# Two sums of modulation rows in the even layer, moved from TensorE to VectorE

## The chip, the core and the metric

One core of one Trainium2 chip runs one program. The metric is the device time of one execution in microseconds (us). The kernel before has a median of 1068.35 us over three runs (1067.42 to 1072.57). A second figure is the span of one profiled execution, from which all rows below come: 1067.8 us, in an execution that took 1069.53 us.

## What is computed

The reference is a trunk of two layers over 512 tokens of width 1024. What bears on the change is the modulation: for each layer `c_act @ ada_w[layer] + ada_b[layer]` gives 6144 numbers, which are cut into `shift1, scale1, gate1, shift2, scale2, gate2`.

```python
mod = c_act @ ada_w[layer] + ada_b[layer]
shift1, scale1, gate1, shift2, scale2, gate2 = jnp.split(mod, 6, axis=-1)
h = modulate(rmsnorm(x, norm1_w[layer]), shift1, scale1)
...
x = x + gate1[:, None, :] * mix
h2 = modulate(rmsnorm(x, norm2_w[layer]), shift2, scale2)
ffn = hier_moe(h2, ...)
x = x + gate2[:, None, :] * ffn
```

Layer 0 (the even one) mixes by pooling and by chunked attention with eight heads; layer 1 by a state space mixer. After each mixer come 32 experts, of which each token uses two.

## The kernel before

The tokens lie in four tiles of 128. A layer's modulation is made in three parts of 2048 columns by the generator `ada(layer, part, eng)` (line 171): part 0 is shift1 and scale1, part 1 gate1 and shift2, part 2 scale2 and gate2. A part reads a weight matrix of 1024 x 2048 in eight tiles `ada` of 128 x 2048 (1 MB each, line 188), two ahead, and ends a step (`yield`) per tile.

There are two ways to add up. With `eng=None` TensorE multiplies each tile by a column of `ccol` (the activated c), four matmuls a tile into four groups of 32 rows of one PSUM bank (`ada_mm`, line 168). With an engine given, that engine makes a running sum: the first tile times its column of `ccol` (line 204), then each next tile times its column plus the sum so far (line 202), in place. TensorE then multiplies the last tile by ones (line 212), four matmuls in all. `SLACK` (1) empty steps lie between the last sum and this product. Then a bias is added (line 215), and the rows go to DRAM (`modd`) or, in part 0, through transposes `pm` (`mod_cols`, line 306) into columns.

In the even layer the parts (0,1), (0,2) and (1,0) are made beside the attention. `even_mixer` writes its work in one order: projections `pdq`, `pdk`, `pdu` (three passes of matmuls, 24 for each 128 columns), scores `sc` with their softmax on VectorE and ScalarE, transposes `ptr` of the probabilities, values `po`, pooling `py`, and last the output projection `mo`. Between these pieces `fill()` takes so many steps of the generators as the table `FILL` says. Tile then sets a fixed order for each engine from this program order, its dependencies and its buffers; each engine runs that order. The softmax of one pair of heads is eight tiles, each with an addition of the bias with a row maximum (line 685), a negation (687), an exponential on ScalarE (688), a reciprocal (689) and a product (690), giving `pr`.

The tiles `ada` have five buffers (`W8`), which the experts' first weights use after them. A tile's buffer is free when its last reader is done: before, the matmuls of that tile; with a running sum, the sum of the next tile. All loads are issued by SyncE's queue in one fixed order, and a load that waits for its buffer holds what is queued behind it.

After part (0,2) the router's weights are scaled (line 251), for which `mc` is read back from `modd` (line 244). After part (1,0) the row buffer of its bias is free, and `gate1` is loaded into it (line 463); the rows of the output projection's weights are multiplied by it (line 492) and split into a high and a low half (`mow0h` on ScalarE, `mow0l` on VectorE, lines 111 and 112) before `mo` can start. Behind `mo` lie the router and the experts of layer 0, then layer 1.

Of the kernel before, what the change touches and what calls it, by code (L numbers as in the profile page):

```python
# [51 lines left out]
SLACK = 1  # L52
# [24 lines left out]
def trunk_kernel(ctx, tc, x, c, ada_w, ada_b, norm1_w, norm2_w, mix_w_in, pool_w, pool_scale,  # L77
# [4 lines left out]
    V, S, GP, PE, SP = nc.vector, nc.scalar, nc.gpsimd, nc.tensor, nc.sync  # L82
# [7 lines left out]
    def w8(shape, name):  # L90
        return wp.tile(shape, F32, tag="w8", name=name, bufs=W8)
# [10 lines left out]
    def ps(shape=(P, 512), name="ps"):  # L102
        return pp.tile(list(shape), F32, tag="ps", name=name)

    def load_after(ins, first):

        if first is not None:
            tc.add_manual_dep(ins.ins, first.ins.name, SYNC, reason="load_after")
# [56 lines left out]
    def ada_mm(p, k, w, first, last):  # L165

        for q in range(4):
            PE.matmul(p[32 * q:32 * q + 32, :], ccol[:, k:k + 1].to_broadcast([P, 32]), w[:, q * 512:(q + 1) * 512],  # L168
                      start=first, stop=last, skip_group_check=True)

    def ada(layer, part, eng, first=None):


        rows = small.tile([P, D], F32, tag="rows", name=f"adab{layer}{part}", bufs=1)
        b = rows[:, 0:512]
        GP.memset(b, 0.0)
        SP.dma_start(b[0:P:32, :], ada_b[layer, part * 2048:(part + 1) * 2048].rearrange("(b n) -> b n", n=512))
        if part == 2:
            router_loads(layer)
            n2 = rows[:, 512:D]  # L180
            GP.memset(n2, 0.0)
            SP.dma_start(n2[0:64:32, :], norm2_w[layer].rearrange("(b n) -> b n", n=512))
        ws = {}

        def load(k):
            if k < KD:
                ws[k] = w8([P, 2048], f"ada{layer}{part}{k}")
                load_after(SP.dma_start(ws[k], ada_w[layer, k * P:(k + 1) * P, part * 2048:(part + 1) * 2048]), first)

        load(0)  # L190
        load(1)
        p = None
        for k in range(KD):
            load(k + 2)
            yield
            if not eng:
                if not k:
                    p = ps(name=f"pada{layer}{part}")
                ada_mm(p, k, ws.pop(k), k == 0, k == KD - 1)
                continue  # L200
            if k:
                a = eng.scalar_tensor_tensor(ws[k], ws[k], ccol[:, k:k + 1], ws[k - 1], op0=ALU.mult, op1=ALU.add)  # L202
            else:
                a = eng.tensor_scalar(ws[0], ws[0], ccol[:, 0:1], None, op0=ALU.mult)
            if k in PIN:
                tc.keep_in_program_order(a)
        for _ in range(SLACK if eng else 0):
            yield
        if eng:
            p = ps(name=f"pada{layer}{part}")  # L210
            for q in range(4):
                PE.matmul(p[32 * q:32 * q + 32, :], ones[:, 0:32], ws[KD - 1][:, q * 512:(q + 1) * 512], start=True,
                          stop=True, skip_group_check=True)
        m = b
        V.tensor_add(m, p, b)
        if part == 0:
            mod_cols(layer, m)
        elif part == 1:
            SP.dma_start(modd[layer, 1], m[0:P:32, :])
        else:  # L220
            SP.dma_start(modd[layer, 2, 2:4], m[64:P:32, :])
            V.scalar_tensor_tensor(n2, m, 1.0, n2, op0=ALU.add, op1=ALU.mult)
            SP.dma_start(modd[layer, 2, 0:2], n2[0:64:32, :])
            yield from router_prep(layer)
# [5 lines left out]
    def router_loads(layer):  # L230
        d = rt[layer] = {"wr": small.tile([P, KD, NLOG], F32, tag="wr", name=f"wr{layer}", bufs=1)}
        d["mc"] = small.tile([P, 2, KD], F32, tag="mc", name=f"mc{layer}", bufs=1)
        d["lb"] = small.tile([P, NLOG], F32, tag="lb", name=f"lb{layer}", bufs=1)
        GP.memset(d["wr"], 0.0)
        GP.memset(d["lb"], -BIG)
        SP.dma_start(d["wr"][:, :, 0:4], moe_w_group[layer].rearrange("(p k) g -> p k g", k=KD))
        SP.dma_start(d["wr"][:, :, 8:NLOG], moe_w_expert[layer].rearrange("(p k) g e -> p k (g e)", k=KD))
        SP.dma_start(d["lb"][:, 0:4], dap(moe_b_group, 4 * layer, [[0, P], [1, 4]]))
        SP.dma_start(d["lb"][:, 8:NLOG], dap(moe_b_expert, 32 * layer, [[0, P], [1, 32]]))

    def router_prep(layer):
        d = rt[layer]
        for q, off in enumerate((4096, 3072)):
            SP.dma_start(d["mc"][:, q, :], dap(modd, layer * 6144 + off, [[KD, P], [1, KD]]))
        for _ in range(SLACK2):
            yield
        p = ps((P, NLOG), name=f"plb{layer}")
        for k in range(KD):
            PE.matmul(p, d["mc"][:, 1, k:k + 1].to_broadcast([P, P]), d["wr"][:, k, :], start=k == 0, stop=k == KD - 1)
        V.tensor_add(d["lb"], p, d["lb"])  # L250
        V.tensor_mul(d["wr"], d["wr"], d["mc"][:, 0, :, None].to_broadcast([P, KD, NLOG]))
# [51 lines left out]
    def mod_cols(layer, m):  # L303
        p = ps((P, 4, P), name=f"pm{layer}")
        for q in range(4):
            PE.transpose(p[:, q, :], m[:, q * P:(q + 1) * P], ident)
        A = ab[:, layer, 0, :].rearrange("p (b q) -> p b q", b=2)
        B = ab[:, layer, 1, :].rearrange("p (b q) -> p b q", b=2)
        V.scalar_tensor_tensor(A, p[:, :, 64::32].rearrange("p q b -> p b q"), 1.0,
                               n1w[layer].rearrange("p (b q) -> p b q", b=2), op0=ALU.add, op1=ALU.mult)  # L310
        V.tensor_copy(B, p[:, :, 0:64:32].rearrange("p q b -> p b q"))
# [201 lines left out]
    def even_mixer(layer):  # L513
        with ExitStack() as es:
# [217 lines left out]
            order = (0, 1, 4, 5, 6, 2, 7, 3)  # L732
            c_hi, c_lo = ({k: cs[n // 2][:, n % 2, q, :] for n, k in enumerate(order)} for q in range(2))

            adas = [ada(0, 1, None), ada(0, 2, None), ada(1, 0, None)]

            fills = iter(FILL)

# [716 lines left out]
    def odd_mixer(layer, prev):  # L1455
        with ExitStack() as es:
# [25 lines left out]
            with ExitStack() as es2:  # L1482
# [246 lines left out]
                def gnorm(g0):  # L1729
# [14 lines left out]
                    for q in range(2):  # L1744
                        b = tmp(f"gb{g0}{q}")
                        GP.partition_broadcast(b, y[64 * q:64 * q + 1, :])  # L1746
                        for e in range(2):
                            m = 2 * (g0 + q) + e
                            V.scalar_tensor_tensor(gT[m], gT[m], nwcol[:, m:m + 1], b, op0=ALU.mult,
                                                   op1=ALU.mult)  # L1750

                a11, a12 = ada(1, 1, V, prev.gathers[HOLD]), ada(1, 2, V, prev.gathers[HOLD])
                fill = [a11] * (9 + SLACK) + [a12] * (10 + SLACK + SLACK2)
                moe = Moe(layer)
# [62 lines left out]
        return moe  # L1817

    moe = odd_mixer(1, even_mixer(0))
    fw = []  # L1820

# [55 lines left out]
```

## Time and profile before

| what | value |
|---|---|
| median of three runs | 1068.35 us |
| the profiled execution | 1069.53 us |
| its span | 1067.8 us |
| TensorE (PE) busy | 975.3 us, 91% |
| VectorE (DVE) busy | 671.4 us, 63% |
| ScalarE (ACT) busy | 441.1 us, 41% |
| GpSimd (POOL) busy | 175.4 us, 16% |
| mean granted TensorE clock | 0.962 of full speed |
| read from and written to HBM | 254.15 MB and 20.11 MB |

Times in the trace count from the span's start. A row of the timeline gives start, duration, engine, line, operation, out<-in and size; in brackets stands how long the engine was idle before it, and what it had waited for. A matmul's end is modelled, so that two starts tell more than a duration. PE runs its matmuls in the order of the program.

### The profile page before, as it was taken

How to read it: one execution, taken by the hardware profiler on the slowest of the kernel's cores; microseconds unless marked ns; L12 is line 12 of the kernel's file. 1: busy time of each engine (PE TensorE's matmuls, PEld its weight loads, DVE VectorE, ACT ScalarE, POOL GpSimd, SP SyncE). 2: the span in 40 equal slices, each digit the busy share in tenths (PEclk: the TensorE clock that was granted, in tenths of full speed). 3: DMA queues.
4: the chain of work that ended last, by engine and by line, in shares of the span. 5: the costliest groups of instructions: out<-in, count | busy, mean ns of one | idle time of the engine just before them, and what ended most of it. 6: DMA issues, size and time to landing. Idle time of an engine off the chain costs nothing. (4 is left out here: it accounts for less than half of the span.)

```text
span 1067.8 us, 15932 instructions
## 1 busy us (share of the span) xinstructions
PE 975.3 (91%) x5700; PEld 722.0 (68%) x5700; DVE 671.4 (63%) x1508; ACT 441.1 (41%) x893; POOL 175.4 (16%) x252
## 2 busy tenths in 40 slices
PE   5889998898799998899999999999959997999993
PEld 4576654687556656778887887888738776665653
DVE  3424444445564875868986889985874555655864
ACT  4334442315122334437675574665532233222332
POOL 3002110304241123400000200100110004321133
PEclk9899999998899999999999999999969997999997
DMA  9689867698599979747884358654338544899987
GB/s 320 215 290 297 292 218 274 244 366 292 196 376 412 411 245 273 242 104 200 254 236 119 108 150 261 213 139 118 99 120 325 204 160 164 280 412 414 410 251 178
DMA packets 137839, 263.87 MB, mean 247 GB/s; under 512 B 17555, under 2 KB 79975, under 8 KB 132632
## 3 DMA queue, kind: packets, MB, share of 16 engines
q1 hardware_dynamic: 126760, 235.36, 63.3%
q0 software_dynamic: 8928, 20.97, 7.5%
q10 hardware_dynamic: 2064, 6.42, 1.5%
q8 instruction: 49, 0.80, 0.3%
q14 instruction: 38, 0.31, 0.1%
HBM read 254.15 MB, written 20.11 MB: 257 GB/s over the span
## 5 line engine op out<-in xcount | busy, mean ns | idle before, releaser
L1063 PE MATMUL ph<-w,xT 128*64 128x256 f32 (+1 forms) x1152 | 132.1, 374 | 1.5 <-DVE xT L1047 1.2
L1063 PEld LDWEIGHTS ph<-w,xT 128*64 128x64 f32 x1152 | 86.6, 139 | 52.6 <-issue 10.8
L1065 ACT ACTIVATE th<-ph 128x128 f32<-128x128 f32 x34 | 9.4, 277 | 156.3 <-PE pht L1074 131.9
L1084 PE MATMUL pyy<-w,hidT 128*64 128x512 f32 x272 | 65.9, 605 | 4.3 <-ACT hidT L1076 3.8
L1049 ACT ACTIVATE xT<-pxt,mc 128x128 f32<-128x128 f32 x136 | 51.1, 457 | 17.3 <-PE pxt L1042 11.8
L1030 POOL DMA_INDIRECT xg<-xnd,toks x32 | 32.2, 1007 | 150.7 <-PE pxt L1042 123.4
L1089 DVE SCALAR_TENSOR_TENSOR y<-pyy,wsl,gate 128x512 f32<-128x512 f32 x68 | 47.9, 742 | 7.0 <-DMA yd<-y 5.4
L1042 PE MATMUL pxt<-ident,xg 128*128 128x128 f32 x272 | 37.9, 284 | 14.8 <-DVEq L1415 8.5
L1066 DVE SCALAR_TENSOR_TENSOR th<-th,ph 128x128 f32<-128x128 f32 x34 | 9.7, 286 | 60.5 <-ACT th L1065 60.5
L1047 DVE TENSOR_SCALAR xT<-pxt,mc 128x128 f32<-128x128 f32 x136 | 46.6, 403 | 1.4 <-PE pxt L1042 1.4
L1042 PEld LDWEIGHTS pxt<-ident,xg 128*128 128x128 f32 x272 | 34.5, 194 | 15.4 <-issue 15.0
L1631 ACT ACTIVATE ms<-lb,acs 128x128 f32<-128x128 f32 x128 | 40.0, 389 | 10.9 <-DMA lb<-acd 10.9
L1115 DVE TENSOR_TENSOR x<-x,pyc 128x512 f32<-128x512 f32 x48 | 30.4, 681 | 21.1 <-DMA x<-yd,row 16.9
L1727 POOL TENSOR_TENSOR gsum<-gsum,sq 128x512 f32<-128x512 f32 x8 | 11.7, 1458 | 188.6 <-ACT sq L1726 166.2
L1595 DVE SCALAR_TENSOR_TENSOR cvx<-pdx,cw,cvx 128x511 f32<-128x511 f32 (+2 forms) x48 | 35.6, 742 | 0.5 <-ACT cvx L1592 0.5
L1084 PEld LDWEIGHTS pyy<-w,hidT 128*64 128x64 f32 x272 | 16.5, 136 | 28.3 <-issue 19.4
L492 DVE TENSOR_TENSOR sor<-sor,gate 128x1024 f32<-128x1024 f32 x16 | 19.9, 1251 | 21.9 <-DMA sor<-in_ssm_w_out_dram 21.9
L1746 POOL PARTITION_BROADCAST gb<-gy x8 | 9.2, 1151 | 147.6 <-DVE gy L1743 139.0
L1210 POOL DMA_INDIRECT x<-yd,row x16 | 25.4, 1590 | 48.1 <-issue 23.9
L202 DVE SCALAR_TENSOR_TENSOR ada<-ada,ccol,ada 128x2048 f32<-128x2048 f32 x14 | 32.8, 2344 | 0.1
L1107 PE MATMUL pyc<-yh,yot 128*128 128x512 f32 x96 | 25.7, 397 | 1.8 <-DVE yot L1097 1.8
L168 PE MATMUL pada<-ada,ccol 128*32 128x512 f32 x192 | 24.9, 600 | 1.1 <-DMA ada<-in_ada_w_dram 1.1
(1086 smaller groups left out, 2662.2 us busy)
## 6 DMA issues: line engine op xcount, KB each, us to landing
w<-in_moe_w_dram SPq DMA_DIRECT2D x192, 512.0 KB
ada<-in_ada_w_dram SPq DMA_DIRECT2D x40, 1024.0 KB
yd<-y SPq DMA_DIRECT2D x22, 512.0 KB
ada<-in_ada_w_dram SPq DMA_DIRECT2D x16, 512.0 KB
wx<-in_ssm_w_in_dram SPq DMA_DIRECT2D x16, 512.0 KB
wz<-in_ssm_w_in_dram SPq DMA_DIRECT2D x16, 512.0 KB
lb<-acd SPq DMA_DIRECT2D x32, 256.0 KB
sor<-in_ssm_w_out_dram SPq DMA_DIRECT2D x16, 512.0 KB
```

The lines of the kernel that those rows point to most:

```text
L202: a = eng.scalar_tensor_tensor(ws[k], ws[k], ccol[:, k:k + 1], ws[k - 1], op0=ALU.mult, op1=ALU.add)
L1030: d = GP.indirect_dma_start(out=xg, out_offset=None, in_=xnd[:, :], in_offset=bass.IndirectOffsetOnAxis(ap=idx, axis=0), bounds_check=T - ...
L1042: PE.transpose(p[:, q, :], xv[:, 4 * hf + q, :], ident)
L1047: V.tensor_scalar(xT[:, k, :], p[:, q, :], a, b, op0=ALU.mult, op1=ALU.add)
L1049: S.activation(xT[:, k, :], p[:, q, :], AF.Identity, bias=b, scale=a)
L1063: PE.matmul(ph[64 * j:64 * j + 64, n:n + h, :], xT[:, k, 64 * j:64 * j + 64], w13[n][:, :, k, :], start=k == 0, stop=k == KD - 1, skip_gro ...
L1084: PE.matmul(py[64 * j:64 * j + 64], hT[:, 64 * j:64 * j + 64], w2[:, s], start=True, stop=True, skip_group_check=True)
L1089: V.scalar_tensor_tensor(y[:, s], py, self.wsl[:, slot:slot + 1], self.gate2[:, s], op0=ALU.mult, op1=ALU.mult)
L1107: PE.matmul(p, part[2][:, i * P:(i + 1) * P], part[hf][:, q * 512:(q + 1) * 512], start=not sums and n + q == 0, stop=stop and n == len(pa ...
L1115: V.tensor_add(xst["x"][i][:, s], xst["x"][i][:, s], p)
L1595: V.scalar_tensor_tensor(a[:, sh:], p[:, :T - sh], cw[:, tap, ch:ch + 1], a[:, sh:], op0=ALU.mult, op1=ALU.add)
L1631: S.activation(ms[:, h, :], lb[:, h, :], AF.Relu, scale=-1.0, bias=acs[:, cq, 4 * g + h:4 * g + h + 1])
```

## The change

`ada` takes the number of empty steps as an argument. Part (0,1) stays on TensorE. Parts (0,2) and (1,0) become running sums on VectorE, with two and three empty steps ahead of their products by ones.

```diff
-    def ada(layer, part, eng, first=None):
+    def ada(layer, part, eng, first=None, slack=SLACK):
...
-        for _ in range(SLACK if eng else 0):
+        for _ in range(slack if eng else 0):
             yield
...
-            adas = [ada(0, 1, None), ada(0, 2, None), ada(1, 0, None)]
+            adas = [ada(0, 1, None), ada(0, 2, V, slack=2), ada(1, 0, V, slack=3)]
```

The three places where the order matters most follow. First, PE behind the scores of the third pair of heads, from the last matmul of the projection `q3` on; `plb` is the router's bias, `ptr` transposes the probabilities of this pair. Before:

```order
L452 MATMUL pdq_1295<-hhi_179,q3l 128x512
L168 MATMUL pada_1054<-ada_1110,ccol 32x512 x4
L168 MATMUL pada_1054<-ada_1138,ccol 32x512 x4
L168 MATMUL pada_1054<-ada_1210,ccol 32x512 x4
L249 MATMUL plb_1340<-wr_960,mc_961 128x40 x8
L168 MATMUL pada_1360<-ada_1354,ccol 32x512 x4
L168 MATMUL pada_1360<-ada_1356,ccol 32x512 x4
L700 MATMUL ptr_1373<-exch,pr_1215 128x128
```

And in the changed kernel:

```order
L452 MATMUL pdq_1279<-hhi_179,q3l 128x512
L212 MATMUL pada_1309<-ada_1194,ones 32x512 x4
L249 MATMUL plb_1320<-wr_960,mc_961 128x40 x8
L700 MATMUL ptr_1340<-exch,pr_1199 128x128
L700 MATMUL ptr_1344<-exch,pr_1199 128x128 x2
```

Five groups of products became one, which reads the last tile of the sum (0,2), `ada_1194`; everything behind it on PE stands in line.

Second, VectorE in the same place, in the changed kernel: the end of the softmax of the third pair (`mx` row statistics, `pr_1199` and `pr_1200` the probabilities of its two heads).

```order
L685 ISA scs_1267,mx_1266<-sc_1264,strip_1196 128x128
L685 ISA mx_1266 128x1
L202 SCALAR_TENSOR_TENSOR ada_1194<-ada_1194,ccol,ada_1125 128x2048
L689 RECIPROCAL mx_1257<-mx_1257 128x1
L687 TENSOR_SCALAR mx_1266<-mx_1266 128x1
L690 TENSOR_SCALAR pr_1199<-scs_1258,mx_1257 128x128
L689 RECIPROCAL mx_1266<-mx_1266 128x1
L690 TENSOR_SCALAR pr_1200<-scs_1267,mx_1266 128x128
L215 TENSOR_TENSOR adab_957<-pada_1309,adab_957 128x512
```

Of the eight sums of part (0,2) the first five stand ahead of this softmax, among the splits `k3l` and `u2l`; two stand inside it and the last one, shown here, has only five small instructions of the softmax behind it.

Third, PE at the end of the attention: the last matmul of the pooling's projection `u3`, then what follows. Before, the eight products of part (1,0) and the transposes `pm` stood ahead of `pdu` of `u2` and `u3`. Now:

```order
L452 MATMUL pdu_1558<-hhi_179,u3l 128x512
L212 MATMUL pada_1599<-ada_1439,ones 32x512 x4
L306 MATMUL pm_1605<-ident,adab_1331 128x128 x4
L700 MATMUL ptr_1612<-exch,pr_1444 128x128
L700 MATMUL ptr_1616<-exch,pr_1444 128x128 x2
```

On VectorE the first three sums of part (1,0) come behind the router's scaled weights (line 251); the second and third are parted by the low half of `po`, and the other five lie inside the fourth pair's softmax, the last of them (`ada_1439`) behind all its products.

## Rows read from the trace of the kernel before

**Rows 1.** The page's first part: engine, busy us, share of the span, instructions.

```profile
PE 975.3 (91%) x5700; PEld 722.0 (68%) x5700; DVE 671.4 (63%) x1508; ACT 441.1 (41%) x893; POOL 175.4 (16%) x252
```

**Rows 2.** Windows: stretch, its length, busy us per engine, PE clock, DMA share, GB/s.

```profile
100.00:125.00 25.00, 25.00 (x140) 16.25 (x142) 11.67 (x48) 11.89 (x28) 3.40 (x3) 1.00 0.90 306
125.00:150.00 25.00, 24.87 (x144) 15.23 (x140) 10.61 (x41) 10.35 (x29) 0.20 (x1) 1.00 0.64 224
150.00:175.00 25.00, 23.89 (x152) 12.37 (x148) 4.87 (x14) 6.47 (x16) 3.08 (x3) 1.00 0.95 358
```

**Rows 3.** Timeline of PE, attention of the third and fourth pair of heads.

```profile
142.97 0.50 PE L449 MATMUL pdq<-hhi,q3h 128*128 128x512 f32 x1
...
148.64 1.92 PE L168 MATMUL pada<-ada,ccol 128*32 128x512 f32 x16
...
151.35 1.98 PE L249 MATMUL plb<-wr,mc 128*128 128x40 f32 x16
153.26 1.92 PE L168 MATMUL pada<-ada,ccol 128*32 128x512 f32 x16
155.11 1.31 PE L700 MATMUL ptr<-exch,pr 128*128 128x128 f32 x10
...
165.34 1.25 PE L700 MATMUL ptr<-exch,pr 128*128 128x128 f32 x10
...
168.51 2.37 PE L711 MATMUL po<-ptT,vsb 128*64 128x512 f32 x14
170.81 1.12 PE L682 MATMUL sc<-kT,qT 64*128 64x512 f32 x2
```

**Rows 4.** Every sum in layer 1: operation, count, duration ns least/median/most.

```profile
L204 DVE TENSOR_SCALAR ada<-ada,ccol x2: 1273/1276/1279, 490.4 to 639.8; 128x2048 f32<-128x2048 f32 x2
L202 DVE SCALAR_TENSOR_TENSOR ada<-ada,ccol,ada x14: 2335/2343/2353, 497.2 to 672.0; 128x2048 f32<-128x2048 f32 x14
```

**Rows 5.** Timeline of DVE: the softmax of the second pair, first and last instruction.

```profile
115.52 0.69 DVE L685 CUSTOM_DVE_ANT_0 scs<-sc,strip 128x512 f32<-128x512 f32 x1
...
123.38 0.29 DVE L690 TENSOR_SCALAR pr<-scs,mx 128x128 f32<-128x128 f32 x1
```

**Rows 6.** Timeline of DVE: router's weights, values of the third pair, and the gate.

```profile
161.59 0.49 DVE L251 TENSOR_TENSOR wr<-wr,mc 128x320 f32<-128x320 f32 x1 [7.42 <-DMA mc<-modd]
171.55 0.69 DVE L112 TENSOR_TENSOR c<-po,c 128x512 fp32r<-128x512 f32 x1 [9.47 <-ACT c L111]
172.16 0.68 DVE L685 CUSTOM_DVE_ANT_0 scs<-sc,strip 128x512 f32<-128x512 f32 x1
...
185.80 1.23 DVE L492 TENSOR_TENSOR mor<-mor,gate 128x1024 f32<-128x1024 f32 x1 [3.26 <-DMA gate<-modd]
```

**Rows 7.** Timeline of PE, from the end of the modulation to the output projection.

```profile
180.59 0.66 PE L306 MATMUL pm<-ident,adab 128*128 128x128 f32 x4 [3.12 <-DVE adab L215]
181.00 0.49 PE L449 MATMUL pdu<-hhi,u2h 128*128 128x512 f32 x1
...
193.60 1.25 PE L700 MATMUL ptr<-exch,pr 128*128 128x128 f32 x10
...
198.84 2.37 PE L711 MATMUL po<-ptT,vsb 128*64 128x512 f32 x14 [1.03 <-ACT ptT L702]
202.94 1.10 PE L664 MATMUL py<-pl,pw 128*128 128x512 f32 x2 [1.74 <-DVE pl L659]
203.48 0.79 PE L457 MATMUL mo<-mow0h,c 128*128 128x512 f32 x1
```

**Rows 8.** Timeline of PE: a long wait in the experts of layer 0.

```profile
273.11 1.94 PE L1042 MATMUL pxt<-ident,xg 128*128 128x128 f32 x8 [8.51 <-DVEq L1415]
```

**Rows 9.** Windows just behind PE's waits of 3.12, 8.51 and 6.19 us.

```profile
181.00:185.00 4.00, 4.00 (x14) 3.18 (x13) 1.03 (x7) 0.49 (x2) 0.00 (x0) 0.57 0.66 148
185.00:190.00 5.00, 5.00 (x24) 4.12 (x23) 1.29 (x2) 1.55 (x2) 0.97 (x1) 1.00 1.01 412
273.00:277.00 4.00, 3.89 (x21) 3.36 (x22) 2.89 (x16) 1.50 (x4) 0.00 (x0) 0.51 0.52 164
790.00:796.00 6.00, 5.71 (x14) 4.51 (x15) 6.00 (x8) 1.71 (x3) 1.12 (x1) 0.52 0.54 175
```

## The prediction
> **What bounds the kernel now.** I read the page's busy shares first: TensorE is busy for 91% of the span, VectorE for 63% [rows 1]. Shares are averages, so next the windows over the attention, 100 to 175 us, where the change is made: PE is busy in 73.76 of 75 us at a granted clock of 1.00, that is its upper level of 2.4 GHz, and DVE in only 27.15 us [rows 2]. A reader who stops here sees an overloaded engine and an idle one. The timeline of PE then gives the price of each piece that stays or goes [rows 3], the groups of layer 1 the price of a sum on DVE [rows 4], and the timeline of DVE where its idle time lies [rows 5, 6]. Last comes the question which wait ends last: the end of this stretch is the first `mo` at 203.48 us, for all behind it follows in order [rows 7].
>
> **What goes and what comes.** A product step on PE is worth 0.93 us: two of them take the 1.85 us from 153.26 to 155.11 [rows 3]. Sixteen go and two products by ones come, each of the same four matmuls: 14 x 0.93 = 13.0 us less for PE. DVE gets two sums, each of one scaled tile at 1.28 us and seven additions at 2.34 us [rows 4]: 17.7 us a sum, 35.3 us in all. DVE had 75 - 27.15 = 47.85 us idle there [rows 2], so the work as such fits. The order is fixed, though, and the product by ones stands in PE's line: what counts is when the last addition ends and where PE has got to by then. I replay both engines by hand.
>
> **Part (0,2) on DVE.** The softmax of the second pair ends at 123.67 us (123.38 + 0.29), 8.15 us after its start at 115.52 [rows 5]. A 512-wide split of 0.69 us [rows 6] now lies inside it: 124.4. Ahead of the next softmax the order puts the scaled tile, four additions and the splits `k3l` and `u2l` (128x1024, 1.23 us, as the row of that size in [rows 6]): 1.28 + 9.36 + 2.46 brings 137.4. The softmax of the third pair takes 8.15, with one more split and the three last additions inside it 15.9 us, to 153.3; behind the last addition stand two reciprocals, a negation and two products of the softmax, some 1.05 us (0.29 for a product and 0.15 to 0.2 for a column, by the spacing in [rows 5]). The sum is ready at **152.2**.
>
> **PE meanwhile.** Rid of five steps it would come to `pdq` of `q3` at 142.97 - 4.6 = 138.4, and the bank for it comes free with the split of the second pair's values at about 138.8. This projection takes 5.67 us (142.97 to 148.64) [rows 3], so PE stands before the product by ones at 144.5 and waits **7.7 us**, a wait that did not exist. Behind it in line are the router's bias, the transposes, `pdk`, and so the fourth pair's scores.
>
> From 152.2 on: product 0.93, `plb` 1.91 (151.35 to 153.26), transposes 1.25, `pdk` 5.67, then 5.47 from the second transposes to the scores (165.34 to 170.81) [rows 3]. This last piece held a product step that goes, but the same sequence without one waits 1.03 us for ScalarE's copy at 198.84 [rows 7], so I leave it. The scores begin at **167.4**, against 170.81 before: 3.4 us early. The 13 us became 3.4.
>
> DVE is not late here. The read back of `mc` held it idle for 7.42 us [rows 6], and behind that wait stand the first sums of (1,0). With the product done at 153.1, the row's two additions of 0.7 and this wait bring 162.0; 0.49 + 1.28 + 2.34 brings 166.1, before the low half of `po` is due (168.51 to 171.55 is 3.04 [rows 3, 6], so 165.1 + 3.04 = 168.1). With the split of 0.69 and the third addition, the softmax starts at 171.2 against 172.16.
>
> **Part (1,0).** That softmax has five additions inside it, and pooling's step of 0.9 (a 512-wide one and a column): 171.2 + 8.15 + 11.7 + 0.9 = **192.0** for the last sum. PE begins `pdu` once the softmax has read its first scores (171.9), does two of them in 11.3 us, and waits from 183.3 to 192.0, **8.7 us**. Before, it waited 3.12 us there, for a bias row queued behind the softmax, and started `pdu` at 181.00 [rows 7]. Then product 0.93, bias and transposes `pm` 0.75 and 0.41: the fourth pair's transposes begin at 194.1 against 193.60. From there to `mo` took 9.88 us (to 203.48). Of this the wait of 1.74 us for pooling goes, whose inputs are done during PE's wait, and some 0.6 of the 1.03: 7.6 us, so `mo` begins at **201.7**, 1.8 us early.
>
> Meanwhile the gate: `pm` to `gate1` landed took 185.80 - 180.59 = 5.2 us [rows 6, 7], so 193.7 + 5.2 = 198.9, and four operations of about 1.2, 1.1, 0.7 and 1.2 us make `mow0l` ready at 203.1. The first matmuls of `mo` want only its high half, so this fits, with nothing to spare.
>
> **The clock.** Behind a wait of 3.12 us PE had 0.57 of its clock for 4 us, behind one of 8.51 us [rows 8] 0.51 for 4 us, behind one of 6.19 us 0.52 for 6 us [rows 9]: a stretch at 1.2 GHz costs (1 - 0.57) x 4 = 1.7, 2.0 and 2.9 us. The change makes two waits of about 8 us, and the first loss passes into the second sum through scores and softmax. I take 2.0 for each, from the wait nearest in length: +4.0. The bounds are 0 (if the half clock falls on work that waits anyway, as ahead of the copy) and 2 x 2.9 = 5.8. The Trainium skill says in "TensorE: Matmul & The Clock Gate", "Part 1: The HAM clock gate", that the throttled state is the default and activity releases it; by it a long wait is paid for a second time, as a slow stretch behind it, and the sum is +2.2 us where without it it would be -1.8. The trace agrees, with 0.57, 0.51 and 0.52.
>
> Sum: -1.8 + 4.0 = **+2.2 us**. With the bounds of the clock it is -1.8 to +4.0; my replay may be off by 3 us more either way, as additions that meet loads and GpSimd may take longer or shorter here than in layer 1, which no row shows. Behind `mo` PE's order is as before, so the shift carries to the end. The profiled execution of 1069.53 becomes 1071.7; it lies 1.18 above the median, which becomes **1070.6**. A measurement tells about 0.5%, 5.3 us, from no change: this is no change.
>
> **Rivals.**
>
> *No waits (faster).* The sums would slip into DVE's idle time and PE would keep its 13.0 us: 1068.35 - 13.0 = 1055.4. For it speaks the room of 47.85 us against 35.3; against it the fixed order, in which the last addition of each sum lies inside a softmax and PE has less left to do before it. It needs the sums done 7.7 and 8.7 us earlier, and only half of that already gives about 1062. I give it 0.10. The Trainium skill's "Perfetto Trace Analysis", "Identifying the Most-Contended Engine", would have the engine of highest occupancy relieved first; by that alone the change brings 1055.4, and no row yet shows a wait that contradicts it.
>
> *The gate is late (slower).* Part (1,0) now ends when the experts' first weights are released by its last additions, and about 1.5 MB of them stand ahead of `gate1` in SyncE's queue. At 412 GB/s, which this place reached [rows 9], they take 3.8 us. `mow0h` then comes 3.8 us later, `mo` waits, and 1068.35 + 2.2 + 3.8 = 1074.4. It decides as soon as the gate lands later than about 199. For it: the loads and the gate share a queue. Against it: part of the weights is issued before the last sum. Chance 0.20.
>
> *The forecast.* Both waits, the half clock, no late gate: 0.64 within 0.5%, with 0.04 on its faster side. The remaining 0.02 is a slower mishap of the clock, past 2 x 2.9.
>
> **How the numbers follow.** Faster 0.10 + 0.04 = 0.14, same 0.64, slower 0.20 + 0.02 = 0.22. The likeliest case alone spans 1065 to 1074: -1.8 to +4.0 gives 1066.5 to 1072.4, and the replay's error adds some 1.5 at either end when the two are not at their worst together. To hold 8 in 10 the range must reach into both rivals: down to 1062, half of the waits, and up to 1077, a late gate with the dearer clock (1074.4 + 1.8, and about 1 more). The predicted time is the likeliest case's.
>
> **What would show it.** In the trace of the changed kernel, the product by ones at line 212 should stand behind waits of 7 to 9 us, twice, ended by VectorE's additions of line 202 at about 152 and 192 to 196. The windows behind each should show a granted clock near 0.5 for some 4 us. DVE should still idle about 7 us at `mc`. `mo` should begin at about 205.7 (201.7 and the two slow stretches). If the waits are under 3 us, or the clock stays at 1.00 behind them, the forecast is too slow; if DVE waits for `gate` past 199 and PE for `mow0h`, the second rival holds. An addition that takes 3 us in place of 2.34 would make each wait some 4 us longer and the forecast wrong by more than 0.5%.

## The result, and the profile of the changed kernel

The changed kernel takes 1074.08 us in the median of 11 runs, the kernel before 1068.35 us in as many. The ratio is 1.0062, with a 95% interval of 1.0040 to 1.0084: slower by 4 to 9 us, or 0.6%. That lies inside the range given, 3.5 us above the forecast of 1070.6, and just past the 0.5% that the prediction counted as no change. One of the changed kernel's runs (1153.88 us) was disturbed and is left out of the ratio. The profiled execution took 1075.62 us, with a span of 1073.9 us, so it lies 6.1 us above that of the kernel before in both.

The first part of the page, which answers to [rows 1]:

```profile
PE 965.3 (90%) x5588; PEld 724.0 (67%) x5588; DVE 706.8 (66%) x1524; ACT 441.7 (41%) x893; POOL 178.0 (17%) x252
```

TensorE is busy for 10.0 us less (13.0 was worked out, at the full clock), VectorE for 35.4 us more (35.3 was worked out), and the program is longer. The timeline of PE, which answers to [rows 3] and [rows 7], shows where it stands still; in brackets are the idle time and what ended it. Each of the four matmuls of a product step leaves two records, hence x8:

```profile
152.27 1.93 PE L212 MATMUL pada<-ada,ones 128*32 128x512 f32 x8 [8.42 <-DVE ada L202]
154.13 3.64 PE L249 MATMUL plb<-wr,mc 128*128 128x40 f32 x16
157.57 2.38 PE L700 MATMUL ptr<-exch,pr 128*128 128x128 f32 x10
165.45 1.25 PE L700 MATMUL ptr<-exch,pr 128*128 128x128 f32 x10
...
169.92 2.43 PE L682 MATMUL sc<-kT,qT 64*128 64x512 f32 x16
...
194.12 1.93 PE L212 MATMUL pada<-ada,ones 128*32 128x512 f32 x8 [8.68 <-DVE ada L202]
196.92 1.09 PE L306 MATMUL pm<-ident,adab 128*128 128x128 f32 x4 [0.86 <-issue]
197.80 2.34 PE L700 MATMUL ptr<-exch,pr 128*128 128x128 f32 x10
...
204.66 2.37 PE L711 MATMUL po<-ptT,vsb 128*64 128x512 f32 x14
207.12 1.20 PE L457 MATMUL mo<-mow0h,c 128*128 128x512 f32 x4
```

The two products by ones stand behind waits of 8.42 and 8.68 us, both ended by VectorE's additions. The rows behind each take about twice as long as elsewhere: `plb` 3.64 us instead of 1.98, the transposes 2.38 and 2.34 instead of 1.31 and 1.25. The windows say why. Their columns are those of [rows 2]; the clock is the number after POOL. Behind the first wait:

```profile
140.00:150.00 10.00, 3.85 (x17) 2.83 (x16) 9.91 (x27) 4.21 (x13) 2.34 (x1) 0.83 0.78 277
150.00:155.00 5.00, 2.73 (x12) 1.06 (x13) 3.76 (x8) 0.83 (x4) 0.20 (x1) 0.50 0.85 267
155.00:160.00 5.00, 5.00 (x24) 5.00 (x25) 0.89 (x2) 1.17 (x4) 0.53 (x1) 0.50 0.81 292
160.00:170.00 10.00, 10.00 (x52) 7.04 (x51) 4.04 (x3) 2.50 (x6) 0.00 (x0) 0.99 0.50 178
```

and behind the second:

```profile
195.00:200.00 5.00, 4.14 (x23) 3.11 (x16) 0.93 (x3) 1.15 (x3) 4.44 (x4) 0.50 0.96 356
200.00:205.00 5.00, 5.00 (x19) 2.20 (x20) 2.90 (x6) 3.33 (x8) 0.00 (x0) 0.88 0.60 213
```

The granted clock is 0.50, the lower of the two levels, from inside the wait to 160 us, 8 us after the first wait has ended, and to some 201 us, 7 us after the second. VectorE, meanwhile, is busy for 9.91 of 10 us between 140 and 150 us. In the kernel before, the softmax and a split kept it busy for 8.16 there; two additions now lie in this stretch as well:

```profile
140.00:150.00 10.00, 9.87 (x59) 6.45 (x60) 8.16 (x39) 4.73 (x17) 0.00 (x0) 1.00 0.31 108
```

In the changed kernel VectorE's timeline, answering to [rows 6], with the last additions of both sums (149.88 and 191.73):

```profile
149.88 2.34 DVE L202 SCALAR_TENSOR_TENSOR ada<-ada,ccol,ada 128x2048 f32<-128x2048 f32 x1
...
161.40 0.49 DVE L251 TENSOR_TENSOR wr<-wr,mc 128x320 f32<-128x320 f32 x1 [3.39 <-DMA mc<-modd]
...
171.26 2.34 DVE L202 SCALAR_TENSOR_TENSOR ada<-ada,ccol,ada 128x2048 f32<-128x2048 f32 x1
...
191.73 2.34 DVE L202 SCALAR_TENSOR_TENSOR ada<-ada,ccol,ada 128x2048 f32<-128x2048 f32 x1
...
203.83 2.36 DVE L492 TENSOR_TENSOR mor<-mor,gate 128x1024 f32<-128x1024 f32 x2
...
207.10 1.23 DVE L112 TENSOR_TENSOR mow0l<-mor,mow0h 128x1024 fp32r<-128x1024 f32 x1 [0.25 <-ACT mow0h L111]
```

The sums are ready at 152.2 and 194.1 us. The gate's rows are scaled as soon as VectorE has done what is ahead of them: nothing waits for the load of `gate1`, although SyncE issues it only at 198.04 us (181.28 before).

So `mo` begins at 207.1 us against 203.48, 3.6 us late. The other 2.5 us of the 6.1 come behind it. In the kernel before, the experts' first products run at half clock for 4 us [rows 9]; these are the windows from 277 us on:

```profile
277.00:281.00 4.00, 2.82 (x27) 2.03 (x26) 3.07 (x15) 0.00 (x0) 1.61 (x2) 1.00 0.31 112
281.00:285.00 4.00, 4.00 (x35) 3.67 (x33) 0.79 (x5) 0.66 (x3) 0.36 (x1) 1.00 0.76 248
```

and in the changed kernel:

```profile
277.00:281.00 4.00, 3.09 (x16) 2.39 (x16) 2.64 (x15) 0.89 (x3) 0.00 (x0) 0.50 0.52 157
281.00:285.00 4.00, 2.70 (x16) 1.65 (x17) 2.80 (x11) 0.00 (x0) 1.53 (x2) 0.50 0.33 117
285.00:289.00 4.00, 4.00 (x35) 3.83 (x32) 0.78 (x5) 0.28 (x1) 0.45 (x1) 0.81 0.52 152
```

The same work in the same order met the lower clock for some 11 us instead of 4. PE's timeline at the start of this work (`pxt`) and behind it (`pwsl`) has, in the kernel before, `pxt` at 273.11 us [rows 8] and

```profile
282.10 1.96 PE L1389 MATMUL pwsl<-wrw,w 128*128 128x16 f32 x16
```

and in the changed kernel

```profile
275.21 1.94 PE L1042 MATMUL pxt<-ident,xg 128*128 128x128 f32 x8 [7.56 <-DMA xg<-xnd,toks]
...
287.57 1.96 PE L1389 MATMUL pwsl<-wrw,w 128*128 128x16 f32 x16
```

so `pxt` is 2.1 us late and `pwsl` 5.5 us.

### The profile page after: what moved, and what is told of

Read it like the earlier page. It is cut to its first block, busy times and chain, and to the rows that moved or that the text cites. A ratio compares the mean times of both kernels' runs of the same rounds, so it can differ in the third digit from the quotient of the medians.

```text
span 1073.9 us, 15735 instructions
## 1 busy us (share of the span) xinstructions
PE 965.3 (90%) x5588; PEld 724.0 (67%) x5588; DVE 706.8 (66%) x1524; ACT 441.7 (41%) x893; POOL 178.0 (17%) x252
## 5 line engine op out<-in xcount | busy, mean ns | idle before, releaser
L1063 PE MATMUL ph<-w,xT 128*64 128x256 f32 (+1 forms) x1152 | 134.3, 378 | 2.6 <-DVE xT L1047 1.5
L202 DVE SCALAR_TENSOR_TENSOR ada<-ada,ccol,ada 128x2048 f32<-128x2048 f32 x28 | 65.7, 2345 | 0.2
L1727 POOL TENSOR_TENSOR gsum<-gsum,sq 128x512 f32<-128x512 f32 x8 | 15.5, 1941 | 186.0 <-ACT sq L1726 164.2
L688 ACT ACTIVATE scs<-scs,mx 128x512 f32<-128x512 f32 (+3 forms) x32 | 17.9, 560 | 31.5 <-DVE mx L687 29.6
```

What stands on the lines that cost most here:

```text
L1063: PE.matmul(ph[64 * j:64 * j + 64, n:n + h, :], xT[:, k, 64 * j:64 * j + 64], w13[n][:, :, k, :], start=k == 0, stop=k == KD - 1, skip_gro ...
```

## The experiments

Three theories went in. **A**: the saved products are given back at the two products by ones, each of which waits for a sum that ends inside a softmax, and in the half clock behind each wait. **B**: VectorE's added work costs as such, wherever it stands. **C**: the experts' loads and the gate, displaced by part (1,0), are what costs. The first four runs shared runs of the kernel before with a median of 1066.48 us, the next four 1067.21, the last four 1067.29. Ratios are to these.

### One part alone

```diff
-            adas = [ada(0, 1, None), ada(0, 2, V, slack=2), ada(1, 0, V, slack=3)]
+            adas = [ada(0, 1, None), ada(0, 2, V, slack=2), ada(1, 0, None)]
```

> Part (0,2) as a sum on VectorE, part (1,0) back on TensorE. Theory A (the saved products are given back at the two products by ones, each of which waits for a sum that ends inside a softmax, and in the half-clock stretch behind each wait): one wait of about 8.4 us ended at 152.3 us by the last addition, a clock near 0.5 for 4 to 8 us behind it, so the fourth pair's scores at about 175 us (before 170.8); the row's bias then finds VectorE free because two projections lie ahead of it, and mo begins at 200 to 203 us: 1064 to 1069 us, 5 to 10 below the changed kernel. Theory B (the loss is VectorE's added work as such, wherever it stands): half of the loss goes, about 1071 us. Theory C (the experts' loads and the gate, displaced by part (1,0), are what costs): the loss is gone wholly, 1062 us or below, with mo before 199 us.

Measured: 1064.88 us, ratio 0.9974 (0.9953 to 0.9996). The wait of 8.43 us stands before 152.06 us as in the changed kernel, `mo` begins at 202.3 us. As theory A had it, in the wait, in `mo` and in the time. B, which wanted 1071 us, and C, which wanted 1062 or below, miss.

```diff
+            adas = [ada(0, 1, None), ada(0, 2, None), ada(1, 0, V, slack=3)]
```

> Part (1,0) as a sum on VectorE, part (0,2) back on TensorE. Theory A: no wait at 152 us; one of about 4 to 5 us before the product by ones, ended near 189 us, and a second of about 3 us before the transposes of the modulation, since the bias row is queued behind the softmax; mo at 204 to 206 us: 1069 to 1072 us. Theory B: half of the loss, about 1071 us, with the softmax longer by the additions in it. Theory C: the whole loss stays, 1074 us or more, with VectorE waiting for gate past 200 us.

Measured: 1063.68 us, ratio 0.9961 (0.9944 to 0.9979), `mo` at 199.2 us. PE's timeline:

```profile
185.00 1.93 PE L212 MATMUL pada<-ada,ones 128*32 128x512 f32 x8 [5.75 <-DVE mx L689]
188.49 1.11 PE L306 MATMUL pm<-ident,adab 128*128 128x128 f32 x4 [1.55 <-DVE adab L215]
```

The two waits are there (the last addition ends at 184.85 us; the view names an instruction of the softmax beside it), but the sum is ready 4 us and `mo` begins 5 to 7 us earlier than I had expected, and all three theories miss the time. C is out: it wanted the whole loss to stay. My own slip: I counted two products of (1,0) ahead of the fourth pair's scores, and the order has five there. Without a wait at 152 us in front, their 4.6 us reach the fourth softmax, and the sum with it.

This is the more telling result: each part alone is faster than the kernel before, and both together slower. If VectorE's added work cost as such, the two should add up. Under A they compound: the first wait and its half clock delay the fourth softmax, in which the second sum lies.

### Covering the waits

```diff
+            for n in range(warm):
+                PE.matmul(p[0:32, :], ones[:, 0:32], wv[0][:, n % NT, :], start=True, stop=True,
+                          skip_group_check=True)
```

> The changed kernel, with 24 and 28 idle products of a ready tile by ones ahead of the two products by ones, in the bank that these overwrite: TensorE is busy for about 5.6 and 6.5 us of its two waits, nothing else differs. Theory A with its clock: the waits still end at 152.3 and about 192 us (the additions are where they were), but shorter, 2 to 3 us each, and the clock behind them is 0.9 to 1.0, so mo begins at 202 to 204 us and the time is 1068 to 1071 us. If the clock is not part of the loss: mo at 207 us and 1074 us. If idle products cost more than the clock gives: over 1076 us.

Measured: 1094.81 us, ratio 1.0261 (1.0225 to 1.0296). It failed as an experiment. The first 24 idle products took 20.4 us, not 5.6, in PE's timeline:

```profile
142.69 20.36 PE L214 MATMUL pada<-vsb,ones 128*32 128x512 f32 x47
```

That is 0.85 us each, as if one after the other: all wrote the same 32 rows of the bank, while the four of a product step write four groups of rows and take 0.93 us together. With TensorE busy throughout, no wait was left there, and the clock stayed at 1.00 from 142 to 174 us. Spread over the groups:

```diff
-                PE.matmul(p[0:32, :], ones[:, 0:32], wv[0][:, n % NT, :], start=True, stop=True,
+                q = n % 4
+                PE.matmul(p[32 * q:32 * q + 32, :], ones[:, 0:32], wv[0][:, n % NT, :], start=True, stop=True,
```

> The idle products of the run before, now spread over the four groups of 32 rows of the bank in turn (24 and 28 of them, so 6 and 7 times four). In the run before all went to one group and took 0.85 us each, one after the other; four in four groups took 0.93 us together in every other row. So now 5.6 and 6.5 us inside the two waits. Theory A with its clock: both waits still end at about 152.3 and 192 us, 2 to 3 us long, and the clock behind them stays over 0.9; the scores of the fourth pair come at 167 to 168 us in place of 169.9, mo at 201 to 204 us, 3 to 6 us below the changed kernel (1066 to 1070 us on this chip). If the clock is not part of the loss: mo at 207 us, 1072 us.

Measured: 1074.41 us, ratio 1.0076 (1.0057 to 1.0095), `mo` at 206.2 us. The first wait in PE's timeline, and windows behind it and, last, behind the second:

```profile
142.79 5.36 PE L215 MATMUL pada<-vsb,ones 128*32 128x512 f32 x48
...
151.33 1.06 PE L218 MATMUL pada<-ada,ones 128*32 128x512 f32 x8 [2.84 <-DVE ada L204]
```

```profile
152.00:154.00 2.00, 2.00 (x12) 1.68 (x9) 1.10 (x3) 0.00 (x0) 0.20 (x1) 0.59 0.81 218
154.00:156.00 2.00, 2.00 (x12) 2.00 (x12) 0.45 (x2) 0.19 (x1) 0.00 (x0) 0.50 0.76 317
...
196.00:198.00 2.00, 1.61 (x9) 1.61 (x10) 0.57 (x3) 0.40 (x2) 1.92 (x2) 0.69 1.00 346
198.00:200.00 2.00, 2.00 (x9) 1.48 (x8) 0.00 (x0) 1.35 (x3) 1.45 (x2) 0.50 0.79 317
```

The idle products fit and the waits shrink to 2.84 and 2.97 us; they end at 151.3 and 194.5 us (152.3 and 194.1 in the changed kernel). The clock falls all the same, only later: at 152 us, to come back at 159, and behind the second wait for some 3 us, from 197 to 200. The scores of the fourth pair begin at 168.25 us, 1.7 us earlier than in the changed kernel, 0.9 of it because the first sum itself was ready earlier; at `mo` 0.9 us is left, and the time gains nothing. So the run does not part the clock from the waits, because a wait under 3 us, too, was followed by the half clock.

### Moving the product

```diff
-FILL = (0, 1, 5, 0, 1, 0, 1, 1, 1, 2, 1, 0, 0, 1, 0, 5, 4, 0, 0, 1, 1, 1, 4, 0, 12)
+FILL = (0, 1, 5, 0, 1, 0, 1, 1, 1, 2, 1, 0, 0, 1, 0, 4, 5, 0, 0, 1, 1, 1, 4, 0, 12)
```

> The changed kernel with one step moved in the table of steps, so that the product by ones of part (0,2) and the router's bias come one piece later, behind the first transposes of the third pair. Theory A as I hold it (the additions have pushed the softmax itself to 153.3 us, so the transposes have to wait as long as the product had): the wait of about 8 us stays and is now before the transposes, ended by the probabilities pr at about 153.5 us; mo at 206 to 208 us, 1072 to 1076 us. Rival (the product by ones stands too early in TensorE's line, the work behind it could run): the wait shrinks to under 3 us, mo is 4 to 8 us earlier, 1066 to 1070 us.

Measured: 1075.95 us, ratio 1.0083 (1.0060 to 1.0105), `mo` at 211.8 us. PE's timeline:

```profile
150.19 0.90 PE L700 MATMUL ptr<-exch,pr 128*128 128x128 f32 x3 [5.71 <-DVE pr L690]
153.38 1.12 PE L700 MATMUL ptr<-exch,pr 128*128 128x128 f32 x4 [2.29 <-DVE pr L690]
...
198.48 1.93 PE L212 MATMUL pada<-ada,ones 128*32 128x512 f32 x8 [10.57 <-DVE ada L202]
```

The wait of 5.71 + 2.29 = 8.0 us is still there and has another name: the transposes now wait for the probabilities, which the additions in the softmax made late. The rival falls. `mo` came 4 us later than expected, because the second sum did: the half clock lasts to some 165 us here, the row is finished later, `mc` is used at 166.7 us in place of 161.4, and the additions queued behind it end at 198.3 us.

### Freeing VectorE of the wait for `mc`

```diff
-        V.tensor_mul(d["wr"], d["wr"], d["mc"][:, 0, :, None].to_broadcast([P, KD, NLOG]))
+        (V if layer else GP).tensor_mul(d["wr"], d["wr"], d["mc"][:, 0, :, None].to_broadcast([P, KD, NLOG]))
```

> The changed kernel with the scaling of the router's weights (line 251) on GpSimd, so that VectorE no longer waits about 4 to 7 us for mc ahead of the additions of part (1,0). Theory A: five of these additions now come before the fourth softmax, the last one ends at 187 to 189 us in place of 194.1, TensorE's second wait is 3 to 5 us in place of 8.7, mo begins at 201 to 203 us: about 5 us below the changed kernel, 1066 to 1069 us on this chip. The first wait stays 8.4 us. Rival (VectorE's idle time at mc costs nothing, since the fourth softmax waits for its scores anyway): the last addition ends where it did, 1072 us or more.

Measured: 1067.74 us, ratio 0.9997 (0.9984 to 1.0010). PE's two waits:

```profile
151.40 1.93 PE L212 MATMUL pada<-ada,ones 128*32 128x512 f32 x8 [8.44 <-DVE ada L202]
186.26 1.82 PE L212 MATMUL pada<-ada,ones 128*32 128x512 f32 x8 [3.78 <-DVE ada L202]
```

The first is untouched, the second lost 4.9 us, and `mo` begins at 199.0 us, 8.1 us earlier; the rival, 1072 us or more, falls. The idle time of VectorE at `mc` had looked harmless in the kernel before, where nothing urgent was queued behind it. The change put a sum there.

### Half sums

The generator gets a number `nd`: VectorE adds the first `nd` tiles, TensorE multiplies the others by their columns into the same bank, and the product by ones of VectorE's sum comes last. The scaling stays on GpSimd.

```diff
+            if k >= nd:
+                if k == nd:
+                    p = ps(name=f"pada{layer}{part}")
+                ada_mm(p, k, ws.pop(k), k == nd, False)
+                continue
...
-            adas = [ada(0, 1, None), ada(0, 2, V, slack=2), ada(1, 0, V, slack=3)]
+            adas = [ada(0, 1, None), ada(0, 2, V, slack=2, nd=4), ada(1, 0, V, slack=3, nd=4)]
```

> Both parts as half sums: VectorE adds the first four tiles, TensorE multiplies the other four by their column, and the product by ones of VectorE's sum comes last; the scaling of the router's weights on GpSimd. No addition lies inside a softmax any more. Theory A: TensorE does ten products instead of sixteen, 5.6 us less, waits nowhere over 2.5 us and keeps its clock; the wait of 3.1 us of the kernel before goes too, since two projections lie ahead of the bias row. mo begins at 193 to 198 us and the time is 5 to 10 us below the kernel before, 1057 to 1062 us. Theory B (VectorE's work as such): 8 additions are left of 16, so half of the loss, about 1069 us.

Measured: 1054.30 us, ratio 0.9878 (0.9863 to 0.9893), `mo` at 188.8 us.

With `nd=5` in both parts:

> The same with five tiles on VectorE and three on TensorE, so eight products instead of sixteen, 7.4 us less on TensorE; one addition of part (1,0) lies inside the fourth softmax, early. Theory A: as above and 1 to 2 us better if the fifth addition hides, mo at 192 to 198 us, 1056 to 1062 us; if it delays the third softmax, equal to the run with four. Theory B: 1070 us.

Measured: 1052.20 us, ratio 0.9860 (0.9839 to 0.9881), `mo` at 186.2 us. With four or five of a part's eight tiles on VectorE, the kernel beats the one before by 13 and 15 us, more than expected (1057 to 1062 and 1056 to 1062 us). The longest waits of PE between 100 and 210 us with five and three, in the view of its waits (total, times, longest, in us):

```profile
PE pm L312 <- DVE adab L221: 0.8, 1, 0.8
PE mo L464 <- DVE mow0l L112: 0.6, 1, 0.6
PE sc L688 <- DVE mx L691: 0.3, 1, 0.3
```

No wait of a microsecond is left, and the granted clock is 1.00 in every window from 140 to 205 us.

### Order and work apart

In all runs with sums on VectorE, part (1,0) ends behind the last two projections. This run has that order alone, with all sums on TensorE:

```diff
-FILL = (0, 1, 5, 0, 1, 0, 1, 1, 1, 2, 1, 0, 0, 1, 0, 5, 4, 0, 0, 1, 1, 1, 4, 0, 12)
+FILL = (0, 1, 5, 0, 1, 0, 1, 1, 1, 2, 1, 0, 0, 1, 0, 5, 2, 0, 0, 1, 1, 1, 5, 1, 12)
```

> The kernel before with nothing but two steps of the table moved: the last products of part (1,0) and the transposes of the modulation come behind the two last projections, as in every run with half sums; all sums stay on TensorE. It parts the gain of the half sums into order and work. If the order is worth what its waits in the trace of before were (3.1 us before the transposes of the modulation, about 1.7 us of half clock behind them, 1.7 us for pooling): 5 to 6 us below the kernel before, mo at 197 to 199 us, and the half sums' remaining 7 to 9 us are TensorE's fewer products. If the order is worth nothing: within 2 us of before, mo at 202 to 204 us.

Measured: 1061.58 us, ratio 0.9950 (0.9928 to 0.9972), `mo` at 196.4 us. So 5.7 us come from two steps of the table: the waits of 3.12 and 1.74 us shrink to 0.8 and 0.3, and the half clock behind the first goes. From there to five and three `mo` gains 10.2 us, of which eight products less are 7.4, and a wait of 1.2 us for a tile's load, which order alone still has, goes too.

This run is also the base for the two single parts, whose part (1,0) ends behind the projections as well. Against it, by the ratios, (0,2) on VectorE costs 0.9974 - 0.9950 = 0.2% and (1,0) 0.1%, neither clear of noise, and both together 1.0062 - 0.9950 = 1.1%, some 12 us where the sum of the two is under 4. Their waits compound.

The next run takes the scaling on GpSimd out of five and three again:

```diff
-        (V if layer else GP).tensor_mul(d["wr"], d["wr"], d["mc"][:, 0, :, None].to_broadcast([P, KD, NLOG]))
+        V.tensor_mul(d["wr"], d["wr"], d["mc"][:, 0, :, None].to_broadcast([P, KD, NLOG]))
```

> The run with five tiles on VectorE and three on TensorE, with the scaling of the router's weights back on VectorE: the additions of part (1,0) again stand behind the wait for mc. Theory A: the four last of them lie inside the fourth softmax, whose probabilities are not due before the second projection is done, so little is lost: mo at 187 to 192 us, 8 to 14 us below the kernel before. If the move to GpSimd was what gained: over 1062 us.

Measured: 1061.55 us, ratio 0.9943 (0.9919 to 0.9967), `mo` at 195.2 us: between the two answers, 9 us worse than with the scaling on GpSimd. So half sums without that move are no better than the order alone (0.9950). Of the 2.0% between the changed kernel and five and three, the split gives 1.2% (1.0062 to 0.9943) and the move of the scaling 0.8%; with whole sums the move gave 0.65% (1.0062 to 0.9997). A row of PE shows a wait that I had not named:

```profile
168.29 1.94 PE L168 MATMUL pada<-ada,ccol 128*32 128x512 f32 x8 [6.41 <-DMA ada<-in_ada_w_dram]
```

The additions, late behind `mc`, hold the tiles' five buffers, so the loads of the tiles that TensorE multiplies are late: in SyncE's waits one such load stands for 8.4 us until an addition is done.

```diff
-            adas = [ada(0, 1, None), ada(0, 2, V, slack=2, nd=5), ada(1, 0, V, slack=3, nd=5)]
+            adas = [ada(0, 1, None), ada(0, 2, V, slack=2, nd=6), ada(1, 0, V, slack=3, nd=6)]
```

> Six tiles on VectorE and two on TensorE, scaling on GpSimd: two products fewer on TensorE, 1.9 us, but an addition of part (0,2) now lies in the third softmax and two of part (1,0) stand between the low half of the values and the fourth softmax. Theory A: that softmax, and with it the projection that takes its bank, starts 3 to 5 us later, a wait of 3 to 5 us appears before that projection, and the time is no better than with five: 1052 to 1057 us. Rival (fewer products on TensorE are always better): 1050 us.

Measured: 1061.25 us, ratio 0.9942 (0.9918 to 0.9965), `mo` at 194.8 us. The direction is theory A's, the size is not (1052 to 1057 us was expected): the wait before the projection is 7.97 us, not 3 to 5. VectorE's timeline:

```profile
159.67 4.73 DVE L207 SCALAR_TENSOR_TENSOR ada<-ada,ccol,ada 128x2048 f32<-128x2048 f32 x2
167.97 0.69 DVE L691 CUSTOM_DVE_ANT_0 scs<-sc,strip 128x512 f32<-128x512 f32 x1 [3.57 <-POOL strip L680]
```

The additions end at 164.4 us, and then VectorE waits 3.57 us more for `strip`, the bias of the scores. Its load is issued at 158.94 us, in SyncE's queue behind four tiles' loads, some of which had waited for buffers that late additions held, and it has landed only at 167.7. With five and three the same load is issued at 143.51 us, ahead of those tiles, and nothing waits for it. So a part of this wait is the new order of the queue, and the run does not tell how large a part.

```diff
-            adas = [ada(0, 1, None), ada(0, 2, V, slack=2, nd=5), ada(1, 0, V, slack=3, nd=5)]
+            adas = [ada(0, 1, V, slack=0, nd=4), ada(0, 2, V, slack=2, nd=5), ada(1, 0, V, slack=3, nd=5)]
```

> The run with five and three, with part (0,1) as a half sum too, four tiles on each engine: three products fewer on TensorE ahead of the attention's second pair, 2.8 us. Theory A: no wait on an addition, mo at 183 to 185 us, 1049 to 1051 us. Rival (the tiles' loads, not TensorE, set the pace there, as DMA's share of 0.9 to 1.0 between 100 and 110 us has it): no gain, TensorE waits for the later tiles instead, 1052 us or more.

Measured: 1052.06 us, ratio 0.9858 (0.9821 to 0.9895), `mo` at 185.5 us. Three products less bring 0.7 us at `mo`, and in the time nothing that can be told from five and three. The expected 183 to 185 us was missed by a little. The rival has the time right (1052 us or more) and not the reason: no wait of TensorE for a tile's load shows in the trace. Of the 2.8 us, 1.6 are there at the second pair's scores (111.88 us against 113.44 with five and three); behind them the transposes wait 0.56 us for probabilities, and 0.7 us is left.

## Why the prediction came out as it did

**The sums.** Worked out: ready at 152.2 and 192.0 us, with waits of 7.7 and 8.7 us before the products. Measured: 152.2 and 194.1, waits of 8.42 and 8.68 us. The first is exact, in part by luck: the third pair's softmax began at 136.8 us, 0.6 earlier than replayed, and took 0.8 longer. Otherwise the replay from durations of layer 1 and the fixed order held, and the additions cost no more among loads (2.34 us). One sign missed: VectorE idled 3.39 us for `mc`, not some 7, since the slow `plb` kept it waiting first.

**The scores.** Worked out without the clock: 167.4 us. Measured: 169.92, 2.5 us later. The slow stretch itself cost more than that. From the product by ones to the second transposes the working had 0.93 + 1.91 + 1.25 + 5.67 = 9.8 us, the trace has 165.45 - 152.27 = 13.2, so 3.4 us went to the first slow stretch where the sum had 2.0. The last piece, left at 5.47 us for a wait of 1.03 us that ScalarE's copy had caused elsewhere, took 169.92 - 165.45 = 4.47: that wait did not come, and the allowance hid 1.0 us of the clock. Of the 2.5 us, 2.1 reached the second sum.

**The end.** From the second sum to `mo` the working had 201.7 - 192.0 = 9.7 us without the clock; measured were 207.1 - 194.1 = 13.0, so the second slow stretch cost 3.3 where the sum had 2.0. Together -1.8 + 2.1 + 3.3 = +3.6 us at `mo`, against +2.2. The mis-sized step is the clock: "I take 2.0 for each, from the wait nearest in length". The lower clock began inside the waits and lasted 8 and 7 us beyond them, not 4. The two stretches cost 3.4 and 3.3 us, 6.7 together, past the upper bound of 5.8; that `mo` still came within the bounds of the sum, +4.0, is owed to the allowance that was not needed. The rule of the Trainium skill ("TensorE: Matmul & The Clock Gate", "Part 1: The HAM clock gate") that the throttled state is the default had pointed the same way; the trace agrees, with 0.50 behind both waits.

**"The shift carries to the end"** is the other step that failed: +3.6 us at `mo` became +6.1 at the end of the profiled execution. The shift had shrunk to 2.1 us at the experts' first product and was 5.5 us behind their start, where the half clock lasted longer. That stretch varies by itself: from `mo` to the end it took 864.3 us in the kernel before, 866.8 in the changed one, and 860.1 to 868.2 us in the twelve experiments, with no relation to how early `mo` began (867.0 at 199.0, 864.3 at 186.2). The medians, 5.7 us apart, say that it was no accident of one execution. Whether it is tied to this change, or to the moment at which the experts happen to begin, stays open.

**The rivals.** *No waits* did not happen in the changed kernel, but a gain of that size is there: the half sums get 13 to 15 us, with the order and the scaling on GpSimd included. *The gate is late* did not happen: VectorE took up `mor` without a wait for it, and `mow0h` was ready at 207.07, as `po` ended. "Nothing to spare" held, at a later time. The run that moved only the end of the second sum had `mo` 8.1 us earlier without touching the gate.

**Not seen** was that the change brought two things of opposite sign. Moving the end of part (1,0) behind the projections gains 5.7 us alone; the whole sums on VectorE cost 1.1%, some 12 us, against that order. The forecast had the first in it, as the wait of pooling and that of the bias row, and did not name it as a version worth having.

## What to carry to other kernels

Before moving work to an idle engine, replay both engines in their fixed order up to the instruction that needs the result; an engine that is idle for half of a stretch can still deliver eight microseconds late, and two such deliveries in a row compound. Splitting a sum between both engines, so that the idle engine's share ends before the work that sits behind it in line, turned a loss of 6 us into a gain of 6 here, and a gain of 15 once the scaling that held VectorE up had gone to a third engine as well. A running sum in place also holds its buffers until the next addition, so a late addition stalls the loads in a shared queue, and with them the instructions that need the later tiles.

## What was unexpected of the hardware

Four 128x512 products into four groups of 32 rows of a bank take 0.93 us together; 24 of the same size into one group took 0.85 us each. And in the run that covered the waits, TensorE had worked at full clock up to a wait of 2.84 us; behind it the clock was 0.59 and 0.50 for some 7 us, about as long as after 8.42 us. Behind the second wait of that run, 2.97 us, it was low for some 3 us. The length of a wait told little of what it cost behind it.
